# One-tile blocks for the first projection and wk, and another split of the PSUM banks, in a two-block network kernel

## The chip, the cores and the metric

The kernel runs on one core of a Trainium2 chip. The metric is the device time of one execution in microseconds (us). Engines are named as the profile names them: PE is TensorE (PEld its weight loads), DVE is VectorE, ACT is ScalarE, POOL is GpSimd, SP is SyncE, which issues the DMAs.

## The reference

256 tokens x of width 2048 and a memory of 256 rows go through two blocks of a network in float32. What the change touches is the first block's beginning:

```
u  = rms_norm(x) @ w_in                        # 2048 -> 42 column tiles of 128
a  = ssd_mixer(u[SSD part])                    # Mamba-2, two chunks of 128 tokens
b  = rwkv7_mixer(u[RWKV part])                 # 16 heads, a recurrence over 256 steps
x  = x + concat(a, b) @ w_out                  # w_outa: mix 0..7, w_outb: mix 8..15
k, v = rms_norm(mem) @ wk, rms_norm(mem) @ wv  # then cross attention, feed-forward
```

The second block (attention, a state-space layer, two more feed-forward matrices) follows; all matrices are streamed from HBM once. The recurrence of the RWKV mixer is computed in chunks, which needs inverses of triangular matrices.

## The kernel before, in words

**The stream.** `gemm` (L482 to L536) goes through one weight matrix after the other, in the order of `SEQ` (L74): w_in, wk, wv, w_outa, w_outb, wq, wo and so on. A matrix is cut into blocks of columns (`CUT_IN`, `CUT_K`, L71), a block into units of 1024 columns per partition, 512 KB each. `fetch` (L447) has SP issue a unit's DMA into one of three raw buffers, `prep` (L463) splits it: ACT casts the high part wh, DVE subtracts for the low part wl (four buffers of each). w_in has 96 units, wk 32, wv 32, w_outa and w_outb 16 each. For each column tile and each of the unit's k-steps TensorE makes the products wh x hi, wh x lo and wl x hi with the split activations; in the first blocks of a matrix (`WIDE`) the first two are one matmul of 512 columns. After its last unit a tile is evicted (`evac`).

**The mixers** run beside the stream as generators. After each tile of a unit `gemm` calls `step` (L419), which lets each generator go one piece on if a clock of the program's own (the meter) has come to its time; so a block of two tiles calls it twice per unit, a block of one tile once. The RWKV mixer has eight pairs of heads in four quarters, one after the other: `rwkv_prep` makes the operands (tiles gb, ga, pb), `rwkv_inv` (from L700) the inverse. There POOL copies ga into D, DVE transposes it to L, POOL does a forward substitution on W with T as its temporary (62 operations for a quarter), DVE transposes W into Wc (L732), and ia, ib, ic, id on TensorE finish it. `rwkv_out` (L777) then makes gkp, kt, b, z, s and y for two chunks and, after the norm of y, yT and the tile mix8 to mix15. The next quarter's substitution needs the T of the one before, which that quarter's ib, ic and id still use.

**The memory.** `hook_in` (L1430) runs after each unit of w_in. In the last ten units it loads and splits the 16 tiles of the memory (mem, mems on ACT and DVE) and has POOL sum their squares (accmem). The row of the memory's norm is made from memss<-ones (a matmul that sums over partitions), a small chain on DVE (memv, memt, memy) and memss<-memy (a matmul that spreads it). `evac_k` (L1509) needs that row: while it is missing, `Rows.__missing__` (L295) steps the mixers. In the same way `gemm` steps them while an activation (mix14, mix15 for w_outb) is missing.

**PSUM.** `banks` (L330) deals eight banks: n to the stream's sums (pool mm), 2 to pairs (pd), 6 - n to the mixers' other tiles (ps). Before, n is `NMM` = 4 from the start.

**The order.** A scheduler puts the program's instructions in a fixed order on each engine, from the order in which the code issues them and its own estimate of when each could run; on the chip each engine keeps that order. A row that waits holds up all rows behind it on its engine.

Of the kernel before, what the change touches and what calls it, by code (L numbers as in the profile page):

```python
# [23 lines left out]
NG, NM, NX = 42, 35, 6  # L24
NT, T2, NTM, KB = 6, 6, 8, 3

NMM, NMB, NMC = 4, 5, 7

WIDE = {"w_in": 8, "w1": 16, "w2a": 4, "w2b": 4, "w2c": 2, "w_out2": 4, "w_up": 22, "w_da": 4, "w_db": 4}


LIVE, OL, LAT, XS = 4, 4, 0.28, 1.0
# [11 lines left out]
def _blocks(widths, k):  # L44

    out, off = [], 0
    nk = k // P
    for w in widths:
        units, kc = [], 1024 // w
        for c in range(0, nk, kc):  # L50
            n = min(kc, nk - c)
            units.append((c, n, off))
            off += P * n * w
        out.append((w, units))
    return out, off


def _flat(w, widths):
# [3 lines left out]
    for width in widths:  # L62
# [5 lines left out]


CUT_D = [512] * 3 + [256, 128, 128]  # L70
CUT_IN = [512] + [256] * 20 + [512]  # L71
CUT_K = [256] * 8
CUT_O = [256] * 8
SEQ = [("w_in", range(len(CUT_IN))), ("wk", range(len(CUT_K))), ("wv", range(4)), ("w_outa", range(len(CUT_O))), ("w_outb", range(len(CUT_O))), ("wq", range(4)), ("wo", range(4)),  # L74
       ("w1", range(6)), ("w2a", range(4)), ("w1", range(6, 11)), ("w2b", range(4)),
# [3 lines left out]
WIDTHS = {  # L79
    "w_in": CUT_IN,  # L80
    "wk": CUT_K, "wv": [512] * 4, "w_outa": CUT_O, "w_outb": CUT_O, "wq": [512] * 4, "wo": [512] * 4,
    "w1": [512] * 16, "w2a": [512] * 4, "w2b": [512] * 4, "w2c": [512] * 4,
# [152 lines left out]
class Meter:  # L235
# [5 lines left out]
    def __init__(self):  # L241
        self.clk = dict.fromkeys(self.FIXED, 0.0)
        self.t = 0.0
# [58 lines left out]
class Net:  # L302
    def __init__(self, ctx, tc, io):
        self.meter = Meter()
        self.tc, self.nc, self.io, self.ctx = tc, Engines(tc.nc, self.meter), io, ctx
        pool = lambda name, bufs, **k: ctx.enter_context(tc.tile_pool(name=name, bufs=bufs, **k))
        self.cp = pool("const", 1)
        self.rawp = pool("raw", RAW)
        self.whp = pool("wh", AHEAD)
        self.wlp = pool("wl", AHEAD)  # L310
        self.gp = pool("g", NG)
        self.ap = pool("act", 16)
        self.mctx = ctx.enter_context(ExitStack())
        self.mp = self.mctx.enter_context(tc.tile_pool(name="m", bufs=NM, side="right"))
        self.tp = pool("tmp", NT)
        self.sp = pool("small", 8)
        self.banks(NMM, "a")
        self.ready, self.raws, self.nraw, self.nunit = [], {}, 0, 0
        self.units, self.dmas = [], []
        for name, blocks in SEQ:  # L320
            allb = _blocks(WIDTHS[name], KDIM[name])[0]
            for b in blocks:
                width, us = allb[b]
                for c0, n, off in us:
                    self.units.append((name, b, width, c0, n, off))
        self.sides, self.nside, self.busy = [], 0, {}
        self.ncell = 0
        self.R, self.C, self.outs = Rows(self), Rows(self), 0
# [153 lines left out]
    def gemm(self, name, acts, evac, blocks=None, moving_w=False, hook=None):  # L482
# [5 lines left out]
        for blk in (range(len(widths)) if blocks is None else blocks):  # L488
            width = widths[blk]
            wide = blk < WIDE.get(name, 0)  # L490
            base = sum(widths[:blk]) // P
# [858 lines left out]
def tile_net(ctx, tc, io, out):  # L1350
    m = Net(ctx, tc, io)
# [45 lines left out]
    ms = None  # L1397
# [24 lines left out]
    def halves():  # L1422
        for n, w in (("w0", 8), ("a0", 8), ("k_a", 8), ("conv_w", 48), ("conv_b", 12)):
            m.half[n] = t = m.cp.tile([P, w], F32, tag="half_" + n, name="half_" + n)
            m.ts(t, m.v(n, 0, w), 0.5, None, ALU.mult, e=nc.gpsimd)
        for n, w in (("mu_pw", 1), ("mu_pa", 1), ("mu_pg", 2), ("mu_r", 8), ("mu_k", 8), ("mu_v", 8)):
            m.half["1-" + n] = t = m.cp.tile([P, w], F32, tag="1-" + n, name="om_" + n)
            m.ts(t, m.v(n, 0, w), -1.0, 1.0, ALU.mult, ALU.add, e=nc.gpsimd)

    def hook_in(cnt):  # L1430
        nonlocal ms
        if cnt == 2:
            nc.sync.dma_start(m.cst, io["cst"])
            m.bones = m.cp.tile([P, P], F32R, tag="bones", name="bonesr")
            m.act(m.bones, m.c("bones"), AF.Copy)
        if cnt == 3:
            nc.sync.dma_start(m.vec, io["vec"])
            halves()
        if cnt < 8:
            for k in (2 * cnt + 6, 2 * cnt + 7):  # L1440
                xs.split(k)
            loads(2)
        j = cnt - 88
        if j == -2:
            ms = Source("mem", m.v("norm_mem_g", 0, 16), "mem", False)
        if j >= -2:
            for k in (2 * j + 4, 2 * j + 5):
                ms.load(k)
        if j >= 0:
            for k in (2 * j, 2 * j + 1):  # L1450
                ms.split(k)

    m.mix = [None] * 16
    m.xbc, m.zs, m.pg = [], [], [None, None]
# [11 lines left out]
    def evac_in(n, ps):  # L1466
# [35 lines left out]
        else:  # L1502
            m.xbc.append(m.ssd_conv(i if kind == "bc" else 4 + i, ps, rB))

    m.gemm("w_in", xs.acts, evac_in, hook=hook_in)
    xs = None
    m.kT = [None] * 16
# [33 lines left out]
    ms = None  # L1541
# [280 lines left out]
```

## Time and profile before

| | |
|---|---|
| median of 3 runs | 2919.66 us (2918.85 to 2920.1) |
| profiled execution | 2919.99 us, span 2917.7 us |
| mean granted clock of TensorE | 0.988 |
| PE, DVE, ACT, POOL busy | 97%, 70%, 49%, 12% of the span |

The profile is of one execution. Busy shares are of the span. A timeline's row has its start, its duration, the engine, the line, the operation and output <- inputs, and in brackets how long the engine had been idle before it and what released it. All helpers' instructions have one line (L266), so rows are read by their tiles' names, with buffer numbers left out.

### The profile page before, as it was taken

Reading aid. Unit: us, or ns where it says so; the run is one execution under the profiler, and the core shown is the slowest. Engines: PE = TensorE matmul, PEld = TensorE weight load, DVE = VectorE, ACT = ScalarE, POOL = GpSimd, SP = SyncE. Lnnn points to the kernel's source line nnn. Section 1 sums busy time; section 2 is a strip of 40 time slices with the busy share of each in tenths; the row PEclk is TensorE's granted clock in tenths of the full one; section 3 lists DMA queues with packets and bytes.
Section 4 is the critical chain, followed back from the end, with each engine's and each line's share of the span. In section 5 each row is a group of like instructions: output and inputs, shape, how many; then the busy total and the mean of one; then the engine's idle time right before and its main releaser. Section 6 shows DMA issues by size and latency. Waiting matters only on the chain.

```text
span 2917.7 us, 50239 instructions
## 1 busy us (share of the span) xinstructions
PE 2840.0 (97%) x19668; PEld 2598.8 (89%) x19668; DVE 2037.5 (70%) x3689; ACT 1423.4 (49%) x2251; POOL 357.4 (12%) x590
## 2 busy tenths in 40 slices
PE   8989998999999999999999989999999999999998
PEld 7989898799999889988888989999988888888887
DVE  7977885567668675565666788887777665577655
ACT  6554643344454554454455535453555444444444
POOL 4444352600000000000000051210000000000000
PEclk9999999999999999999999999999999999999999
DMA  6544444454545556566565544455555555555664
GB/s 214 177 141 137 148 155 129 145 185 130 171 148 173 188 182 193 188 188 191 186 192 180 184 148 142 160 159 174 181 188 187 188 188 187 190 187 183 191 188 145
DMA packets 146253, 504.17 MB, mean 173 GB/s; under 512 B 16352, under 2 KB 24800, under 8 KB 146016
## 3 DMA queue, kind: packets, MB, share of 16 engines
q1 hardware_dynamic: 146016, 500.96, 53.7%
q8 instruction: 154, 2.52, 0.3%
q14 instruction: 83, 0.68, 0.1%
HBM read 498.80 MB, written 2.10 MB: 172 GB/s over the span
## 4 chain that ended last, share of the span: by engine, by line
PE 78%; DVE 3%; POOL 1%; issue 1%; ACT 0%; DMA 0%; DVEq 0%; ACTq 0%; POOLq 0%
PE mm_w_up L266 17%; PE mm_w L266 12%; PE mm_w_in L266 7%; PE mm_w2a L266 5%; PE mm_w_db L266 4%; PE mm_w_da L266 4%; PE mm_w2c L266 4%; PE mm_w2b L266 4%; PE mm_wo L266 3%; PE mm_wq L266 3%; PE mm_w_out L266 3%; PE mm_wv L266 2%; PE mm_w_outa L266 2%; PE mm_w_outb L266 2%; PE mm_w_ba L266 2%; PE mm_wk L266 1%
## 5 line engine op out<-in xcount | busy, mean ns | idle before, releaser
L266 PE MATMUL mm_w_up<-xu,wh_w_up 128*128 128x512 f32 x1408 | 487.9, 397 | 0.0
L266 PE MATMUL mm_w_up<-xu,wl_w_up 128*128 128x256 f32 x1408 | 376.6, 280 | 0.0
L266 PE MATMUL mm_w<-xf,wh_w 128*128 128x512 f32 x1024 | 350.6, 392 | 0.0
L266 DVE TENSOR_TENSOR wl_w_up<-raw_w_up,wh_w_up 128x1024 fp32r<-128x1024 f32 x176 | 215.4, 1224 | 148.2 <-ACT wh_w_up L266 147.4
L266 PEld LDWEIGHTS mm_w_up<-xu,wh_w_up 128*128 128x128 f32 x1408 | 256.9, 188 | 54.7
L266 ACT CAST wh_w_up<-raw_w_up 128x1024 fp32r<-128x1024 f32 x176 | 184.8, 1050 | 236.0 <-PE mm_w_up L266 219.5
L266 PE MATMUL mm_w_in<-ins,wh_w_in 128*128 128x256 f32 (+1 forms) x1248 | 287.7, 317 | 5.7 <-DVE ins L266 5.7
L266 ACT CAST wh_w_in<-raw_w_in 128x1024 fp32r<-128x1024 f32 (+1 forms) x189 | 196.8, 1043 | 189.8 <-PE mm_w_in L266 104.4
L266 DVE TENSOR_TENSOR wl_w_in<-raw_w_in,wh_w_in 128x1024 fp32r<-128x1024 f32 (+1 forms) x189 | 241.7, 1283 | 57.2 <-ACT wh_w_in L266 56.7
L266 PEld LDWEIGHTS mm_w_up<-xu,wl_w_up 128*128 128x128 f32 x1408 | 265.6, 189 | 9.8
L266 PE MATMUL mm_w<-xf,wl_w 128*128 128x256 f32 x1024 | 273.4, 280 | 0.0
L266 PE MATMUL mm_w_in<-xb,wh_w_in 128*128 128x256 f32 x1472 | 268.4, 284 | 1.1 <-DVE in L266 1.1
L266 DVE TENSOR_TENSOR wl_w<-raw_w,wh_w 128x1024 fp32r<-128x1024 f32 x128 | 156.8, 1225 | 122.0 <-ACT wh_w L266 120.4
L266 PEld LDWEIGHTS mm_w_in<-xb,wh_w_in 128*128 128x128 f32 x1472 | 226.7, 190 | 5.7 <-issue 2.3
L266 PEld LDWEIGHTS mm_w_in<-ins,wh_w_in 128*128 128x128 f32 x1248 | 207.8, 194 | 17.6 <-DVE ins L266 5.7
L266 PEld LDWEIGHTS mm_w<-xf,wh_w 128*128 128x128 f32 x1024 | 186.8, 188 | 35.9
L266 PE MATMUL mm_w_in<-ins,wl_w_in 128*128 128x256 f32 x768 | 215.2, 288 | 2.4 <-DVE wl_w_in L266 2.4
L266 PE MATMUL mm_w_in<-xb,wl_w_in 128*128 128x256 f32 x736 | 206.3, 284 | 2.2 <-DVE wl_w_in L266 2.2
L266 ACT CAST wh_w<-raw_w 128x1024 fp32r<-128x1024 f32 x128 | 134.3, 1049 | 144.2 <-PE mm_w L266 123.0
L266 PEld LDWEIGHTS mm_w<-xf,wl_w 128*128 128x128 f32 x1024 | 192.4, 188 | 7.0
L266 PEld LDWEIGHTS mm_w_in<-ins,wl_w_in 128*128 128x128 f32 x768 | 149.0, 194 | 6.7 <-DVE wl_w_in L266 3.6
L266 POOL TENSOR_TENSOR tt<-st,st 128x256 f32<-128x256 f32 x16 | 13.9, 868 | 1081.9 <-DVE acc L266 1081.5
(1523 smaller groups left out, 7445.7 us busy)
## 6 DMA issues: line engine op xcount, KB each, us to landing
raw_w_in<-in_w_in_dram SPq DMA_DIRECT2D x187, 512.0 KB, 3.6
raw_w_up<-in_w_up_dram SPq DMA_DIRECT2D x176, 512.0 KB, 3.9
raw_w<-in_w_dram SPq DMA_DIRECT2D x128, 512.0 KB, 4.2
raw_w2a<-in_w2a_dram SPq DMA_DIRECT2D x48, 512.0 KB, 4.2
raw_w_da<-in_w_da_dram SPq DMA_DIRECT2D x44, 512.0 KB, 3.9
raw_w_db<-in_w_db_dram SPq DMA_DIRECT2D x42, 512.0 KB, 4.1
raw_w2b<-in_w2b_dram SPq DMA_DIRECT2D x40, 512.0 KB, 4.1
raw_w2c<-in_w2c_dram SPq DMA_DIRECT2D x40, 512.0 KB, 4.2
```

The source lines that it names most:

```text
L266: return f(o, *a, **k)
```

## The change

w_in: one block of 512 columns, then 40 of 128 and two of 256, in place of one of 512, 20 of 256 and one of 512. wk: one of 256 and 14 of 128, in place of eight of 256. The number of units stays, and `WIDE` is set so that the same 18 tiles are wide. The stream's sums have four banks in the first block and three from the second on; the mixers' pool ps gets two and then three. The 16 memory tiles are split behind units 92 to 95, four tiles behind each, in place of 88 to 95, two behind each, and loaded accordingly later.

```diff
--- before.py
+++ after.py
@@ -24,9 +24,9 @@
 NG, NM, NX = 42, 35, 6
 NT, T2, NTM, KB = 6, 6, 8, 3
 
-NMM, NMB, NMC = 4, 5, 7
-
-WIDE = {"w_in": 8, "w1": 16, "w2a": 4, "w2b": 4, "w2c": 2, "w_out2": 4, "w_up": 22, "w_da": 4, "w_db": 4}
+NMM, NMB, NMC = 3, 5, 7
+
+WIDE = {"w_in": 15, "w1": 16, "w2a": 4, "w2b": 4, "w2c": 2, "w_out2": 4, "w_up": 22, "w_da": 4, "w_db": 4}
 
 
 LIVE, OL, LAT, XS = 4, 4, 0.28, 1.0
@@ -68,8 +68,8 @@
 
 
 CUT_D = [512] * 3 + [256, 128, 128]
-CUT_IN = [512] + [256] * 20 + [512]
-CUT_K = [256] * 8
+CUT_IN = [512] + [128] * 40 + [256] * 2
+CUT_K = [256] + [128] * 14
 CUT_O = [256] * 8
 SEQ = [("w_in", range(len(CUT_IN))), ("wk", range(len(CUT_K))), ("wv", range(4)), ("w_outa", range(len(CUT_O))), ("w_outb", range(len(CUT_O))), ("wq", range(4)), ("wo", range(4)),
        ("w1", range(6)), ("w2a", range(4)), ("w1", range(6, 11)), ("w2b", range(4)),
@@ -314,7 +314,7 @@
         self.mp = self.mctx.enter_context(tc.tile_pool(name="m", bufs=NM, side="right"))
         self.tp = pool("tmp", NT)
         self.sp = pool("small", 8)
-        self.banks(NMM, "a")
+        self.banks(4, "a")
         self.ready, self.raws, self.nraw, self.nunit = [], {}, 0, 0
         self.units, self.dmas = [], []
         for name, blocks in SEQ:
@@ -1429,6 +1429,8 @@
 
     def hook_in(cnt):
         nonlocal ms
+        if cnt == 7:
+            m.banks(NMM, "n")
         if cnt == 2:
             nc.sync.dma_start(m.cst, io["cst"])
             m.bones = m.cp.tile([P, P], F32R, tag="bones", name="bonesr")
@@ -1440,15 +1442,15 @@
             for k in (2 * cnt + 6, 2 * cnt + 7):
                 xs.split(k)
             loads(2)
-        j = cnt - 88
+        j = cnt - 92
         if j == -2:
             ms = Source("mem", m.v("norm_mem_g", 0, 16), "mem", False)
-        if j >= -2:
-            for k in (2 * j + 4, 2 * j + 5):
+        for b in range(2 * j, 2 * j + 2) if j >= 0 else (j,) if j >= -2 else ():
+            for k in (2 * b + 4, 2 * b + 5):
                 ms.load(k)
-        if j >= 0:
-            for k in (2 * j, 2 * j + 1):
-                ms.split(k)
+            if b >= 0:
+                for k in (2 * b, 2 * b + 1):
+                    ms.split(k)
 
     m.mix = [None] * 16
     m.xbc, m.zs, m.pg = [], [], [None, None]
```

The change moves instructions. Three places are shown as the rows of an engine in their order; a name's last number is the buffer's, a row with x2 stands for two instructions alike.

TensorE, first projection's end and wk (mm_wk_B_T is the sum of tile T in block B, memss the memory's norm, yT, sg, ss, ic and pb pieces of the mixers). Before, around memss<-memy:

```order
L266 MATMUL mm_wk_1_0_5234<-mems12_4901,wh_wk_1_12_5281 128x256 x2
L266 MATMUL mm_wk_1_0_5234<-mems12_4901,wl_wk_1_12_5282 128x256
L266 MATMUL mm_wk_1_0_5234<-mems13_4907,wh_wk_1_12_5281 128x256
L266 MATMUL ic1_5020<-Q1_4428,ga20_2362 64x64 x2
L266 MATMUL ic1_5020<-Q1_4428,ga21_2363 64x64
L266 MATMUL pb6_4892<-cst_98,v6_4134 128x128 x2
L266 MATMUL ic1_5020<-Q1_4428,ga21_2363 64x64
L266 MATMUL ic1_5020<-Q1_4428,ga30_2532 64x64 x2
L266 MATMUL ic1_5020<-Q1_4428,ga31_2533 64x64 x2
L266 MATMUL memss_5133<-cst_98,memy_5139 128x128 x2
L266 MATMUL mm_wk_1_0_5234<-mems13_4907,wh_wk_1_12_5281 128x256
L266 MATMUL mm_wk_1_0_5234<-mems13_4907,wl_wk_1_12_5282 128x256
```

Now, around the same row:

```order
L266 MATMUL yT1_5015<-pg0h_537,lorg1h_4790 128x256
L266 MATMUL yT1_5015<-pg0l_538,lorg1h_4790 128x256
L266 MATMUL yT1_5015<-pg0h_537,lorg1l_4791 128x256
L266 MATMUL yT1_5015<-pg1h_556,lorg1h_4790 128x256
L266 MATMUL yT1_5015<-pg1l_557,lorg1h_4790 128x256
L266 MATMUL yT1_5015<-pg1h_556,lorg1l_4791 128x256
L266 MATMUL sg1ss_5168<-ones_99,sacc1_4984 128x1 x2
L266 MATMUL memss_4862<-cst_98,memy_4868 128x128 x2
L266 MATMUL ss5_5282<-cst_98,kq5_5109 128x2 x2
L266 MATMUL mm_wk_1_0_4919<-mems0_4360,wh_wk_1_0_4773 128x256 x2
L266 MATMUL mm_wk_1_0_4919<-mems0_4360,wl_wk_1_0_4774 128x256
```

Before, block 1 of wk lies around memss<-memy and between it and memss<-ones (53 rows earlier). Now memss<-ones is 42 rows earlier; between lie the last eight rows of block 0 and then pieces of the mixers alone, and block 1 begins behind it.

TensorE, the last quarter of the RWKV mixer. Before, its ic3 stands between w_outa's tiles:

```order
L266 MATMUL mm_w_outa_3_0_7822<-mix3_7402,wh_w_outa_3_0_7746 128x256 x2
L266 MATMUL mm_w_outa_3_0_7822<-mix3_7402,wl_w_outa_3_0_7747 128x256
L266 MATMUL ic3_7836<-Q3_7449,ga60_4997 64x64 x2
L266 MATMUL ic3_7836<-Q3_7449,ga61_4998 64x64 x2
L266 MATMUL ic3_7836<-Q3_7449,ga70_6531 64x64 x2
L266 MATMUL ic3_7836<-Q3_7449,ga71_6532 64x64 x2
L266 MATMUL mm_w_outa_3_1_7823<-mix0_7349,wh_w_outa_3_0_7746 128x256 x2
L266 MATMUL mm_w_outa_3_1_7823<-mix0_7349,wl_w_outa_3_0_7747 128x256
```

Now it comes in w_outb's block 0, behind the products with mix12 and mix13:

```order
L266 MATMUL mm_w_outb_0_1_8103<-mix12_8032,wl_w_outb_0_4_8063 128x256
L266 MATMUL mm_w_outb_0_1_8103<-mix13_8079,wh_w_outb_0_4_8062 128x256 x2
L266 MATMUL mm_w_outb_0_1_8103<-mix13_8079,wl_w_outb_0_4_8063 128x256
L266 MATMUL ib3_8173<-Q3_8118,T3_7203 32x32 x16
L266 MATMUL ib3_8173<-T3_7203,Q3_8118 32x32 x8
L266 MATMUL ic3_8201<-Q3_8118,ga60_5559 64x64 x2
L266 MATMUL ic3_8201<-Q3_8118,ga61_5560 64x64 x2
L266 MATMUL ic3_8201<-Q3_8118,ga70_6937 64x64 x2
L266 MATMUL ic3_8201<-Q3_8118,ga71_6938 64x64 x2
L266 MATMUL gkp60_8227<-rh6_5244,ka6_5241 128x128 x2
```

Before, ib3 to yT7 are spread from w_outa's block 1 to w_outb's block 1, three sums of w_outb being begun by then. Now the 73 rows from ib3 to yT7 are one run, and the next row of the stream is w_outb's product with mix14.

DVE, behind the second quarter's transpose Wc1 (gk, ce, m, zh are mixers' operands, wl the low part of a unit). Before:

```order
L266 STREAM_TRANSPOSE Wc1_4426<-W1_3392 128x1024
L266 SCALAR_TENSOR_TENSOR zh2_3836<-mm_w_in_18_0_3703,row_in_490 128x256
L266 TENSOR_TENSOR ce6_3814<-ce6_3814,xbc3_1447 128x256
L266 TENSOR_TENSOR m6_3809<-m6_3809,cbm_1455 128x512
L266 TENSOR_TENSOR gk010_3847<-gkp01_3840,cst_98 128x256
L266 SCALAR_TENSOR_TENSOR gk010_3847<-gkp01_3840,nn0_1107,cst_98 128x128
```

Now:

```order
L266 STREAM_TRANSPOSE Wc1_5187<-W1_3911 128x1024
L266 TENSOR_TENSOR wl_w_in_42_4_4277<-raw_w_in_42_4_4189,wh_w_in_42_4_4276 128x1024
L266 TENSOR_TENSOR m7_4219<-m7_4219,cbm_1429 128x512
L266 TENSOR_TENSOR wl_w_in_42_8_4321<-raw_w_in_42_8_4239,wh_w_in_42_8_4320 128x1024
L266 SCALAR_TENSOR_TENSOR zh4_4293<-mm_w_in_41_0_4163,row_in_490 128x256
```

Before, the first row behind Wc1 that TensorE needs next is gk010, four rows on; now it is wl_w_in_42_4, directly behind. The same holds for Wc2 (wl_wv_0_10, directly behind); behind Wc0 it is wl_w_in_23_8, eight rows on (before xe0, six on), behind Wc3 gk410, five rows on.

## Rows read from the trace of the kernel before

**Rows 1.** The page's first part: engine, busy us, share, instructions.

```profile
PE 2840.0 (97%) x19668; PEld 2598.8 (89%) x19668; DVE 2037.5 (70%) x3689; ACT 1423.4 (49%) x2251; POOL 357.4 (12%) x590
```

**Rows 2.** Waits of TensorE, 0 to 900 us: total us, times, longest.

```profile
PE b L266 <- DVE gk L266: 20.8, 3, 8.9
...
PE st L266 <- DVE xe L266: 7.7, 1, 7.7
...
PE gb L266 <- DVE M L266: 1.3, 1, 1.3
```

**Rows 3.** Timeline of DVE: first and last of the four transposes Wc.

```profile
171.18 1.25 DVE L266 STREAM_TRANSPOSE Wc<-W 128x1024 f32<-128x1024 f32 x1 [8.52 <-POOL W L266]
...
570.45 1.25 DVE L266 STREAM_TRANSPOSE Wc<-W 128x1024 f32<-128x1024 f32 x1 [10.57 <-POOL W L266]
```

**Rows 4.** Timeline of TensorE: the four long waits, and id ahead of three.

```profile
175.22 0.77 PE L266 MATMUL st<-xe,btok 128*128 128x128 f32 x2 [7.72 <-DVE xe L266]
...
248.07 1.14 PE L266 MATMUL id<-M,Q 64*64 64x64 f32 x16
...
305.48 0.69 PE L266 MATMUL b<-vt,gk 128*128 128x64 f32 x2 [5.93 <-DVE gk L266]
...
393.59 1.14 PE L266 MATMUL id<-M,Q 64*64 64x64 f32 x16
...
450.97 0.69 PE L266 MATMUL b<-vt,gk 128*128 128x64 f32 x2 [8.86 <-DVE gk L266]
...
516.21 1.14 PE L266 MATMUL id<-M,Q 64*64 64x64 f32 x16
...
573.19 1.28 PE L266 MATMUL b<-vt,gk 128*128 128x64 f32 x4 [6.03 <-DVE gk L266]
```

**Rows 5.** Windows: length, PE, PEld, DVE, ACT, POOL busy, granted clock, DMA share, GB/s.

```profile
175.00:178.50 3.50, 3.28 (x15) 3.31 (x16) 3.50 (x9) 3.44 (x8) 1.21 (x3) 0.50 0.62 192
...
691.00:694.00 3.00, 2.66 (x13) 2.69 (x14) 0.97 (x4) 0.24 (x2) 0.00 (x0) 0.50 0.03 5
...
700.00:704.00 4.00, 4.00 (x33) 4.00 (x32) 2.51 (x6) 2.64 (x5) 0.00 (x0) 0.91 0.00 0
```

**Rows 6.** Timeline of TensorE at the memory's norm and at the mixers' end.

```profile
391.57 0.71 PE L266 MATMUL memss<-cst,memy 128*128 128x128 f32 x4
...
648.11 0.49 PE L266 MATMUL gkp<-rh,ka 64*128 64x128 f32 x4
...
685.19 0.39 PE L266 MATMUL y<-al,gk 128*128 128x64 f32 x2
...
685.59 0.40 PE L266 MATMUL mm_w_outb<-mix,wh_w_outb 128*128 128x256 f32 x2
...
685.95 0.40 PE L266 MATMUL mm_w_outb<-mix,wh_w_outb 128*128 128x256 f32 x2
...
687.77 0.69 PE L266 MATMUL yT<-cst,ka 128*128 128x128 f32 x2 [0.59 <-DVE ka L266]
...
691.34 0.45 PE L266 MATMUL yT<-cst,ka 128*128 128x128 f32 x1 [2.18 <-DVE ka L266]
...
696.30 0.80 PE L266 MATMUL mm_w_outb<-mix,wh_w_outb 128*128 128x256 f32 x2 [1.10 <-DVE xin L266]
```

**Rows 7.** Timeline of DVE at the memory's norm.

```profile
382.62 0.15 DVE L266 TENSOR_SCALAR memv<-memss 128x2 f32<-128x2 f32 x1
...
387.47 0.42 DVE L266 TENSOR_TENSOR bon<-pb,v 128x256 f32<-128x256 f32 x1 [0.19 <-PE pb L266]
...
387.81 0.15 DVE L266 SCALAR_TENSOR_TENSOR memy<-memt,memy 128x2 f32<-128x2 f32 x1
```

**Rows 8.** Groups on DVE, 300 to 400 us: busy us, mean ns, idle before.

```profile
L266 DVE TENSOR_TENSOR wl_wk<-raw_wk,wh_wk 128x1024 fp32r<-128x1024 f32 x9 | 11.5, 1278 | 0.8 <-ACT wh_wk L266 0.8
...
L266 DVE SCALAR_TENSOR_TENSOR mems<-mem,vec,mems 128x256 fp32r<-128x256 f32 x16 | 10.6, 660 | 0.1
...
L266 DVE TENSOR_TENSOR gk<-gkp,cst 128x256 f32<-128x256 f32 x6 | 2.5, 411 | 0.0
```

## The prediction

> **What bounds the kernel.** I read first the busy shares: TensorE (PE) is busy 97% of the span, the next engine, VectorE (DVE), 70% [rows 1]. So the time is TensorE's work, which the change leaves as it is (as many units, matmuls, weight loads), plus what TensorE stands idle, plus what it runs at its lower clock. Second, the waits of TensorE in the first 900 us, the stretch that the change reorders: four waits hold 28.5 us, one at st for DVE's xe (7.7) and three at b for DVE's gk (20.8) [rows 2]. Third, the timelines around them. DVE stands in its queue at the transpose Wc<-W of a mixer's quarter, 8 to 12 us each time, until GpSimd (POOL) has finished the substitution W [rows 3]; what stands behind Wc in DVE's queue is late, and TensorE stops at the first of its rows that reads it. The last three quarters start when the quarter before has done id: from id's start to the row that waited there are 57.4, 57.4 and 57.0 us, in which TensorE had 51.5, 48.5 and 51.0 us of work [rows 4]. This length is POOL's and DVE's, and the change touches none of it. Last, the clock: behind such a wait the granted clock is 0.50, the 1.2 GHz level, for 3.5 us; behind the small waits at the mixers' end it is 0.50 too, and 0.91 again in 700 to 704 us [rows 5].
>
> The profiled execution took 2919.99 us, 0.3 above the median of the runs, so sums against it stand for the median too. 0.2% is 5.8 us; less than that a measurement of this kernel hardly tells from no change.
>
> **The change, part by part.** Blocks of one tile, the split of the wide tiles (18 before and after) and the later memory loads change no instruction's shape and no count. A k-step of three matmuls stays 0.36 us (685.59 to 685.95) [rows 6], a unit of eight 2.9 us. DMA: the 16 memory tiles of 128 KB come within four units in place of eight, and on SP's queue stand between weight units that are fetched three ahead; I count nothing for it, and 1 us if a unit lands late. The change of banks after block 0 makes block 1 wait for another old bank's eviction: 0 to 1 us, taken as 0. The price is in the order.
>
> *The four waits.* With one step of the mixers per one-tile block, a quarter spans other work. I price TensorE's rows from id to the first row that needs DVE's work behind Wc, at 0.36 us a k-step and the mixers' own rows at their spacing in the trace. Second quarter: 48.6 us before, 50.0 now. Third: 44.2, now 54.2. Fourth: 49.5, now 54.3. For the first, from the unit at which DVE reaches L: 51.4, now 55.3. So the waits lose 3.9, 1.4, 10.0 and 4.8 us. But the row that waits now reads a weight split (wl), not a small operand: behind Wc0 eight DVE rows come before it (4 us more), behind Wc1 and Wc2 one split (0.8 more each), behind Wc3 five rows (2 more). New waits: 7.7 - 3.9 + 4 = 7.8; 5.9 - 1.4 + 0.8 = 5.3; 8.9 - 10.0 + 0.8, so 0; 6.0 - 4.8 + 2 = 3.2. That is 16.3 in place of 28.5: **12 us saved**, and 1.8 us more for the wait that goes, half of its 3.5 us at the lower clock: -14. Bounds: nothing, and all 28.5 + 4 x 1.8 = 36.
>
> *The memory's norm.* Here I see the largest new cost. Before, between memss<-ones (the sum) and memss<-memy (the broadcast) TensorE had the end of block 0 of wk and most of a tile of block 1, 7.7 us, with some mixers' rows, and DVE's chain memv to memy took 5.2 us [rows 7]; the broadcast came at 391.57 without a wait [rows 6]. Now three banks are the stream's, block 0 of wk holds two of them until the row of the memory's norm is there, and between the two memss rows stand 1.4 us of wk and 4.6 us of mixers' rows, with no stream row behind ia1 until the broadcast is done. At the same place DVE's queue is denser: the 16 mems now come in four units, right behind Wc1. From Wc1 to memv I count 95 operations: 10 splits at 1.2, 16 mems at 0.66 (their mean beside POOL's adds, against 0.41 of a plain 256-wide one), 26 wide ones at 0.35 (0.34 from one start to the next), 43 small ones at 0.15 [rows 7, 8]: 38 us; from memv to the last memy 49 more, with one split and ten wide ones: 10. With the transpose the broadcast is possible some 50 us behind Wc1's start. TensorE starts again 2.5 us behind it, has 32.8 us of work up to the broadcast, and so would be there at 35. **14.5 us idle**, in pieces at memss, sgb0, yT1. Off go the waits that this place has now, of which gb's for M is 1.3 [rows 2]: some 2 in all. The clock falls in such a stretch as it did at 691 to 703 us; I take 1.5 us. Net **+14**; bounds +5 (if mems and adds don't meet, 0.41 each, and half of the small operations overlap) and +20.
>
> *A cluster in wv* (unit 139: z31, y21, y31, ia2, ib2, yT2 and others within 7 us of stream): the handoffs from TensorE to DVE and back take more than the rows between; 0 to 5, taken as +2.
>
> *The mixers' end.* w_outb's block 0 needs mix14 and mix15. Before, the last quarter's pieces from ic3 on were spread among the units of w_outa and w_outb, and the waits were 0.59 and 2.18 at yT and 1.10 at the xin add, 3.9 us [rows 6]. Now 24 pieces from ib3 to yT7 stand in one run with no stream row between, again while block 0 holds two of three banks: 18.4 us of TensorE's rows. The chain through them (ib, ic, id, then b, z, s, y for two chunks, each handed to ACT or DVE and back at about 1 us, DVE with 16 gk operations of 0.4 on the way, and the last y's norm, 5.8 us from its matmul at 685.5 to yT at 691.34 [rows 6]) comes to 28 to 29 us: 10 idle in place of 3.9. **+6**, the lower clock taken as before (about 10 us of it [rows 5]); bounds 0 and +14.
>
> Sum: -14 + 14 + 2 + 6 = **+8 us**: 2919.99 + 8 = 2928, slower by 0.3%.
>
> A rule on the clock speaks against the change. The row shows 0.50 for 3.5 us behind a long wait and for some 10 us around short ones [rows 5], so I took a few us. The Trainium skill, "TensorE: Matmul & The Clock Gate", Part 1, says that the half-rate state is the default and that activity releases it. By that rule the two runs without stream rows, which TensorE fills by two thirds, could stay throttled throughout, and the sum would be nearer the third rival's than mine.
>
> **Rivals.**
> 1. *The waits close* (faster). If the mixers' third bank and smaller steps give TensorE 57 us of its own rows between id and the first row behind Wc in every quarter, all 28.5 us go, with 7 us of lower clock; the runs at the norm and at the end cost half as much, +10, and wv +2: 2919.99 - 35.5 + 12 = 2896; if only three waits close, about 2905. For it: the third and fourth quarter gain 10 and 5 us of rows. Against: the releaser is DVE held by POOL [rows 3], not a bank, and splits now stand behind Wc. It decides at 57 us of rows. Chance 0.21. The Trainium skill, "Perfetto Trace Analysis", Identifying Performance Opportunities, says that the same gap repeating on the engine that should be saturated can mean too few PSUM buffers; by that rule this rival would be the case. The trace's releasers don't agree.
> 2. *They cancel* (no change). If DVE's mems overlap POOL's adds less, the norm costs +6 in place of 14: 2920. For it: DVE idles 30% of the span. Against: in its queue there is no idle place to use. Chance 0.27.
> 3. *The runs are dearer* (slower still). TensorE's 24 us of rows in both runs at 1.2 GHz, a third of it not hidden by the waits, +8, and each wait 2 longer: 2928 + 12 = 2940. Chance 0.12.
>
> **Numbers.** My own forecast, 2926 to 2936, has 0.40. Slower by over 0.2% is it and the third rival, 0.52; within 0.2%, 0.27; faster, 0.21. The range, 2904 to 2942, takes in the milder half of the first rival and most of the third, and the bounds of the norm and the end together.
>
> **What would show it.** In the waits of the changed kernel: mm_w_in or mm_wv waiting for wl behind Wc0 and Wc1 (8 and 5 us), b for gk at one place only; at the norm, sgb, yT and memss waiting for DVE, 12 to 16 us together, with DVE without idle from Wc1 on; at the end, ten or more waits of 0.3 to 3 us from ib to yT7. The forecast falls if TensorE's waits at the norm stay under 6 us, or if the four waits go altogether. In windows of 50 us the granted clock should be lowest there, under 0.90.

## The result and the profile after

The changed kernel takes **2942.5 us** (median of four runs, 2941.5 to 2944.41) against 2919.88 (2918.85 to 2920.69): a ratio of 1.0078, 95% interval 1.0061 to 1.0096, so slower by 0.8%, 22.6 us. The sign was forecast, the size was not: 2928 was said, with 2942 as the upper end. The profiled execution took 2941.5 us, with a span of 2939.7.

The first line of the page already splits the loss. The columns are those of [rows 1].

```profile
PE 2851.5 (97%) x19668; PEld 2607.6 (89%) x19668; DVE 2041.0 (69%) x3689; ACT 1420.2 (48%) x2251; POOL 358.4 (12%) x590
```

TensorE has the same 19668 matmuls as before, and its busy time has grown by 2851.5 - 2840.0 = 11.5 us. The same rows took longer, and that is its clock: the mean granted clock went from 0.988 to 0.982. The span grew by 22.0 us, so the other 10.5 are idle time. Half of the loss is thus invisible in a list of waits.

The waits of TensorE, 0 to 900 us (total us, times, longest), the view of [rows 2]:

```profile
PE mm_w_outa L266 <- DVE xin L266: 8.8, 1, 8.8
PE yT L266 <- DVE ka L266: 8.7, 5, 2.8
PE mm_w_in L266 <- DVE wl_w_in L266: 6.6, 3, 3.3
...
PE mm_w_in L266 <- DVE foldw_in L266: 6.2, 1, 6.2
PE sgb L266 <- DVE memt L266: 3.0, 1, 3.0
PE pb L266 <- DVE ql L266: 2.9, 2, 2.1
PE s L266 <- DVE al L266: 2.5, 2, 1.6
...
PE mm_wv L266 <- DVE wl_wv L266: 2.1, 1, 2.1
PE ib L266 <- DVE T L266: 1.6, 1, 1.6
PE z L266 <- ACT be L266: 1.5, 2, 1.1
```

Of the rows that waited before, b for gk (20.8) and st for xe (7.7) are gone. One long wait is left of four, at xin; there is a new one at foldw_in, and a dozen of 0.4 to 3 us at the norm, in wv and at the mixers' end. The windows of those places (columns as in [rows 5]):

```profile
0.00:50.00 50.00, 30.15 (x146) 24.12 (x147) 34.23 (x51) 32.31 (x67) 28.52 (x57) 0.90 0.69 217
168.00:202.00 34.00, 30.18 (x239) 28.12 (x238) 32.74 (x59) 17.64 (x37) 29.01 (x46) 0.95 0.37 119
338.00:348.00 10.00, 6.45 (x37) 5.69 (x35) 8.95 (x15) 4.49 (x12) 2.52 (x5) 0.66 0.48 162
364.00:396.00 32.00, 25.59 (x187) 24.55 (x186) 29.87 (x133) 15.58 (x39) 10.14 (x18) 0.73 0.27 88
502.00:506.00 4.00, 1.92 (x9) 1.25 (x8) 3.22 (x3) 0.00 (x0) 1.54 (x4) 1.00 0.00 0
524.00:538.00 14.00, 9.94 (x115) 8.64 (x114) 11.13 (x57) 2.88 (x7) 1.78 (x7) 0.64 0.00 1
628.00:642.00 14.00, 5.20 (x33) 4.66 (x31) 5.15 (x9) 1.05 (x1) 6.53 (x16) 0.63 0.23 69
680.00:720.00 40.00, 32.27 (x265) 29.63 (x264) 23.88 (x98) 9.01 (x27) 0.00 (x0) 0.70 0.09 31
```

A window's length less PE's busy time is what TensorE stood idle; its busy time multiplied by one minus the granted clock (the column behind POOL, 0.70 in the last row) is what the lower clock cost. The mean clock of a long window weighs idle time too, so I took both sums over windows of 2 us from 0 to 800 us and added them up by place. This ledger is used for all kernels below; "a+b" is idle plus lower clock, in us, good to some 0.3.

| place | before | after | difference | forecast |
|---|---|---|---|---|
| start, 0 to 50 | 12.3+1.6 | 19.9+1.9 | +7.9 | 0 |
| four waits at Wc | 28.8+8.9 | 18.2+5.9 | -13.6 | -14 |
| memory's norm | 2.2+1.6 | 6.4+6.7 | +9.3 | +14 |
| wv cluster | 0 | 4.1+3.8 | +7.9 | +2 |
| mixers' end | 3.9+4.1 | 7.7+9.3 | +9.0 | +6 |
| small waits elsewhere | 0.6 | 2.2 | +1.6 | 0 |
| all, 0 to 800 us | 48.0+16.2 | 58.5+27.9 | +22.2 | +8 |

The ledger explains the 22.0 us of the span; behind 800 us nothing differs.

**Start.** DVE and TensorE at the change of banks, timelines of the changed kernel, DVE first:

```profile
46.35 0.41 DVE L266 TENSOR_TENSOR foldw_in<-foldw_in,mm_w_in 128x256 f32<-128x256 f32 x1
```

```profile
46.82 0.80 PE L266 MATMUL mm_w_in<-ins,wh_w_in 128*128 128x512 f32 x1 [6.20 <-DVE foldw_in L266]
47.42 0.41 PE L266 MATMUL mm_w_in<-ins,wl_w_in 128*128 128x256 f32 x1
47.63 0.63 PE L266 MATMUL mm_w_in<-ins,wh_w_in 128*128 128x512 f32 x1
```

The foldw_in that TensorE waits for is the eviction (a fold is the addition of a wide tile's two halves) of the last of block 0's four tiles, not of the first. Before, TensorE began block 1 at 40.83 us without a wait, 7.5 us ahead of that last fold:

```profile
40.83 0.48 PE L266 MATMUL mm_w_in<-ins,wh_w_in 128*128 128x512 f32 x1
...
48.30 0.42 DVE L266 TENSOR_TENSOR foldw_in<-foldw_in,mm_w_in 128x256 f32<-128x256 f32 x1
```

Behind the wait the row after a 256-wide product starts 0.21 us behind it (47.42 to 47.63) and not 0.12; the granted clock is 0.50 from 46.8 to 50 us, the 1.2 GHz level.

**The four waits.** DVE's transposes Wc of the first, second and fourth quarter, and the last row of the memory's norm on DVE:

```profile
190.07 1.25 DVE L266 STREAM_TRANSPOSE Wc<-W 128x1024 f32<-128x1024 f32 x1 [1.26 <-POOL W L266]
...
339.06 1.25 DVE L266 STREAM_TRANSPOSE Wc<-W 128x1024 f32<-128x1024 f32 x1 [7.82 <-POOL W L266]
...
387.39 0.15 DVE L266 SCALAR_TENSOR_TENSOR memy<-memt,memy 128x2 f32<-128x2 f32 x1
...
634.70 1.25 DVE L266 STREAM_TRANSPOSE Wc<-W 128x1024 f32<-128x1024 f32 x1 [11.90 <-POOL W L266]
```

From the second quarter on DVE stands 8 to 12 us as before [rows 3], but TensorE has more of its own to do meanwhile. In the first quarter DVE hardly stands: 1.26 us for 8.52. It comes to that Wc 49 us after POOL began the substitution (139.98 us), in place of 41.5, when POOL is almost done. From the second Wc to the last memy are 387.54 - 339.06 = 48.5 us.

**Norm and end.** TensorE's waits at both, in order of time:

```profile
378.69 1.20 PE L266 MATMUL sgb<-cst,sg0y 128*128 128x128 f32 x4 [2.95 <-DVE memt L266]
...
385.70 0.45 PE L266 MATMUL yT<-cst,ka 128*128 128x128 f32 x1 [2.83 <-DVE ka L266]
...
389.43 1.20 PE L266 MATMUL memss<-cst,memy 128*128 128x128 f32 x4
...
693.58 0.49 PE L266 MATMUL s<-al,kbt 128*128 128x128 f32 x2 [1.56 <-DVE al L266]
...
706.47 0.83 PE L266 MATMUL yT<-cst,ka 128*128 128x128 f32 x2 [1.71 <-DVE ka L266]
...
710.24 0.89 PE L266 MATMUL yT<-cst,ka 128*128 128x128 f32 x2 [1.66 <-DVE ka L266]
```

The broadcast memss<-memy takes 1.20 us where it took 0.71 [rows 6], and comes without a wait, 1.9 us after the last memy was done (387.54): TensorE was slow enough that DVE was ready.

### The profile page after: what moved, and what is told of

It is laid out like the page before. It is cut to its first block, busy times and chain, and to the rows that moved or that the text cites. A ratio compares the mean times of both kernels' runs of the same rounds, so it can differ in the third digit from the quotient of the medians.

```text
span 2939.7 us, 50255 instructions
## 1 busy us (share of the span) xinstructions
PE 2851.5 (97%) x19668; PEld 2607.6 (89%) x19668; DVE 2041.0 (69%) x3689; ACT 1420.2 (48%) x2251; POOL 358.4 (12%) x590
## 4 chain that ended last, share of the span: by engine, by line
PE 84%; POOL 7%; DVE 5%; issue 2%; ACT 1%; DMA 1%; SPq 0%; DVEq 0%; POOLq 0%; ACTq 0%
PE mm_w_up L266 17%; PE mm_w L266 12%; PE mm_w_in L266 12%; PE mm_w2a L266 5%; PE mm_w_db L266 4%; PE mm_w_da L266 4%; PE mm_w2c L266 4%; PE mm_w2b L266 4%; PE mm_wo L266 3%; PE mm_wq L266 3%; POOL W L266 3%; PE mm_w_out L266 3%; POOL T L266 3%; PE mm_wk L266 2%; PE mm_wv L266 2%
## 5 line engine op out<-in xcount | busy, mean ns | idle before, releaser
L266 PEld LDWEIGHTS mm_w_in<-ins,wl_w_in 128*128 128x128 f32 x768 | 149.3, 194 | 10.8 <-DVE wl_w_in L266 8.6
L266 PEld LDWEIGHTS mm_w_in<-xb,wl_w_in 128*128 128x128 f32 x736 | 138.3, 189 | 5.3 <-DVE wl_w_in L266 2.7
```

The lines of the kernel that those rows point to most:

```text
L266: return f(o, *a, **k)
```

## The experiments

The theory after the result: three causes, each with its place. The change of banks makes block 1 wait for all of block 0's tiles (start). The cuts make the mixers late against the stream, so that their last pieces come without stream rows around them (wv, end). In such runs the clock falls and costs as much as the waits. The rivals: the three banks themselves cost (a bank is missing where TensorE waits); or one particular wait in the run drops the clock. Every experiment is a single run, beside a run of the kernel before on the same chip (its time stands in brackets), which took 2919.23 to 2922.46 us in the four groups; the changed kernel's own four runs lie 2.9 us apart. So time differences under some 3 us are not read, and the place of the loss in the ledger is what counts. The ledger's sums follow the times within 4 us.

### The change of banks

**The cuts with four banks throughout:** the change, without its third bank for the mixers and without the change of banks.

```diff
-NMM, NMB, NMC = 3, 5, 7
+NMM, NMB, NMC = 4, 5, 7
-        if cnt == 7:
-            m.banks(NMM, "n")
```

> The changed kernel with the stream's four PSUM banks kept throughout, so without the change of banks behind block 0; cuts and memory loads as changed. Theory A (the banks cost: the change of banks itself some 8 us at 40 to 50 us of the trace, and three banks leave the stream nothing to do at the memory's norm and at the mixers' end): the 6.2 us wait of mm_w_in for foldw_in is gone, and the runs without stream rows at the norm and at the end shrink; 2917 to 2928 us. Theory B (the cuts cost: one step of the mixers per one-tile block makes the mixers late, whatever the banks): only the change of banks goes, 2934 us or more, with the waits in wv and at the end as in the changed kernel.

Measured: 2932.2 us (before beside it 2921.28), between the two ranges: 10.9 of the 22.6 us stay, 11.7 go. Start 14.1, as before; norm 5.0; wv nothing; the end 6.5+15.0 = 21.5, the largest of all runs. So the start belongs to the banks, the end to the cuts. The norm (13.1 in the changed kernel) and wv (7.9) need the banks too: with four banks and as many steps as here the norm loses at most 5.0 in any run, and wv nothing.

**The change of banks alone, to the same sizes:** the kernel before (NMM stays 4), its PSUM pools closed and opened again behind the same unit.

```diff
+        if cnt == 7:
+            m.banks(NMM, "n")
```

> The kernel before with the pools of banks closed and opened again, at their old sizes, behind block 0. Theory A: the first tile of block 1 has to wait until all four tiles of block 0 are evicted, 5 to 6 us idle and 2 us at the lower clock at 40 to 50 us: 2926 to 2929 us. Theory B (the wait at 47 us comes from the one-tile block or the smaller pool): no wait there, 2920 us within 2.

Measured: 2927.2 us (2921.28), 5.9 slower, as expected; start 22.9, the end 2.8 and the norm 1.4 less than before, the rest the same. Its waits of TensorE have the row of after:

```profile
PE mm_w_in L266 <- DVE foldw_in L266: 5.1, 1, 5.1
```

Nothing but the closing and opening differs, with as many banks in each pool: the price is the handover, not a bank that is missing.

**The change of banks two units later,** with wk's cut undone:

```diff
-CUT_K = [256] + [128] * 14
+CUT_K = [256] * 8
-        if cnt == 7:
+        if cnt == 9:
```

> The changed kernel with wk in blocks of 256 and the change of banks behind block 1 (one tile in flight) in place of block 0 (four tiles). If the new pools wait for the tiles in flight to be evicted, the wait falls from 6.6 us to 1 to 2 us and the time from 2927 to 2920 to 2923 us. If changing banks costs the same wherever it stands: 2926 to 2929 us.

Measured: 2929.0 us (2922.46): missed. The wait is there again, 5.4 us at foldw_in, a block later, and the start lost 22.5. I had expected that one tile in flight would cost less than four. But its fold stood in DVE's queue behind those of block 0, the last of which came at 50.33 us, and started at 52.34, 5 us behind the tile's last product.

**Three banks from the start,** no change of banks, a first block of three tiles, wk's cut undone:

```diff
-CUT_IN = [512] + [128] * 40 + [256] * 2
-CUT_K = [256] + [128] * 14
+CUT_IN = [384] + [128] * 41 + [256] * 2
+CUT_K = [256] * 8
-        self.banks(4, "a")
+        self.banks(NMM, "a")
-        if cnt == 7:
-            m.banks(NMM, "n")
```

(w_in's wide blocks are 16, and the memory's tiles are split from unit 94 on, to go with it.)

> The kernel of wk_256 (w_in in one-tile blocks, wk as before) with a first block of 384 columns, so that the stream has three banks from the start and the banks are not changed. If the change of banks costs 6 us or more in that kernel too (2927): 2919 to 2922 us, with no wait for foldw_in at 47 us. If a first block of three tiles leaves TensorE idle while x comes in: what it wins is given back before 40 us, 2926 us or more.

Measured: 2925.3 us (2919.23), between the two ranges. Start 18.5, half way. TensorE's timeline shows what is left:

```profile
36.04 0.79 PE L266 MATMUL mm_w_in<-ins,wh_w_in 128*128 128x512 f32 x1 [3.87 <-DVE foldw_in L266]
...
45.87 0.47 PE L266 MATMUL mm_w_in<-ins,wh_w_in 128*128 128x512 f32 x1 [1.09 <-DVE foldw_in L266]
```

With three banks block 1 waits for the fold of the first tile, 3.9 us: DVE is late with the folds at the start in every arrangement, and four banks without a change are what hid it.

### The cuts

**Both cuts undone,** the banks left as changed:

```diff
-CUT_IN = [512] + [128] * 40 + [256] * 2
-CUT_K = [256] + [128] * 14
+CUT_IN = [512] + [256] * 22
+CUT_K = [256] * 8
```

(`WIDE` goes with it, here and wherever w_in's cut changes.)

> The changed kernel with blocks of 256 columns again in w_in (the first of 512 stays, the last 512 stays cut in two) and in wk, eight wide blocks; banks and memory loads as changed. Theory A (banks): the wait behind block 0 stays, and the norm and the end stay bad: 2932 to 2942 us. Theory B (cuts): the four long waits come back as before, and only the 8 us behind block 0 stay: 2924 to 2929 us.

Measured: 2933.4 us (2921.28), in the range of theory A, but the waits are those of theory B. Start 21.7; the four waits are long again (8.9, 8.9, 11.2, 8.0 with their clock); norm 8.9, end 6.1. With the old cuts the banks give nothing back: the mixers' third bank does not shorten the waits, w_in's cut does.

**wk's cut undone:**

```diff
-CUT_K = [256] + [128] * 14
+CUT_K = [256] * 8
```

> The changed kernel with wk in blocks of 256 again. If the losses at the norm, in wv and at the end come from wk's one-tile blocks (half as many steps, so the mixers fall behind and are forced later), they fall by half or more: 2925 to 2932 us. If they come from the banks and from w_in's cut, the time stays at 2938 to 2946 us.

Measured: 2927.3 us (2921.28), 15 us less than the changed kernel. The wv cluster is gone, the end is 4.5+2.4, the waits as in after; the norm, at 12.8, did not fall as I had expected. So behind w_in's cut and the three banks wk's cut is worth 15 us of the 22.

**w_in's cut alone,** on the kernel before:

```diff
-CUT_IN = [512] + [256] * 20 + [512]
+CUT_IN = [512] + [128] * 40 + [512]
```

> The kernel before with only w_in's middle cut to 40 blocks of 128 (first and last block of 512, 15 wide blocks, memory loads, four banks and wk as before). Theory W (w_in's one-tile blocks shorten the four long waits, some 13 us; wk's one-tile blocks and the change of banks cost the rest): 2904 to 2912 us. Theory M (one-tile blocks make the mixers late wherever they stand, so that the waits won are given back in wv and at the end): 2918 to 2930 us, with more than 10 us lost to waits and clock from 660 us on.

Measured: 2922.4 us (2922.46): no difference. The four waits at Wc fall by some 9 us and the norm's 3.8 go, but a handful of smaller waits of 0.5 to 2.2 us (st, wa, pb, z, ys) come in between, some 10 us with their clock, and the end takes 6 more (6.0+8.0).

**wk's cut alone,** on the kernel before:

```diff
-CUT_K = [256] * 8
+CUT_K = [256] + [128] * 14
```

> The kernel before with only wk cut into one block of 256 and 14 of 128. Theory W: the mixers fall behind in wk, and the losses appear in wv and at the end without any other part of the change, 15 us more: 2930 to 2939 us. If wk's cut costs only together with w_in's or with three banks: 2918 to 2925 us.

Measured: 2924.4 us (2922.46): theory W missed; alone it costs 2 (5 by the ledger), not the 15 that it costs behind w_in's cut and three banks. The third wait falls from 10.8 to 6.1 and the end rises to 13.9.

**Four banks and wk's cut undone:** the first experiment with wk's old cut.

```diff
-NMM, NMB, NMC = 3, 5, 7
+NMM, NMB, NMC = 4, 5, 7
-CUT_K = [256] + [128] * 14
+CUT_K = [256] * 8
-        if cnt == 7:
-            m.banks(NMM, "n")
```

> The changed kernel without the change of banks and with wk in blocks of 256: what is left of it is w_in's cut, its last 512 columns as two blocks of 256, and the memory's loads behind the last four units. Theory W: 2932 less 15 of wk's cut, 2915 to 2919 us, above the one with w_in's middle cut alone by what the crowded norm costs (5 to 9 us). If the norm's loss needs three banks: within 3 us of that kernel.

Measured: 2927.9 us (2922.46): missed by 9. Start 14.7 and norm 2.2 are cheap, but the end is 8.5+8.1 = 16.6 and the rest 35.7. Against w_in's middle cut alone it is 5.4 slower: that is the price of the last block's split and the memory's later loads together. Against this kernel the first experiment adds wk's cut, which so costs some 5.5 with four banks, between the 2 alone and the 15 with three.

Two pairs differ by the banks alone: this kernel and the one with wk's cut undone, and the first experiment and the changed kernel. In both the change of banks adds 7 to 8 us at the start and 8 to 11 at the norm, and takes 7.5 to 8 off the rest (35.7 to 28.0, 34.1 to 26.6) and 10 or 4.5 off the end. So behind w_in's cut the third mixers' bank is worth something, about what the change of banks costs at the start; the norm, and wv where wk is cut, come on top.

### Whether the mixers' lateness sets the end

**A step in the middle of a unit,** in blocks of one tile, so that the mixers get as many calls as with two tiles:

```diff
                             nc.tensor.matmul(o, a, b, start=first and q == 0, stop=last and q == len(ops) - 1)
+                        if nt == 1 and k == m // 2 - 1:
+                            mt.t = mt.now()
+                            self.step()
                     mt.t = mt.now()
```

> The changed kernel with a second step of the mixers in the middle of a unit of a one-tile block, so that a unit calls it twice as before. Theory L (one step per unit makes the mixers late: third id at 579 us in place of 516, so that the last quarter falls into w_outb's block 0): third id before 550 us, the loss in wv (8 us) gone and that at the end down from 17 to 10 us or less; 2924 to 2932 us. If the lateness comes from the order of w_in's tiles and the banks, not from the steps: third id within 10 us of 579, 2938 us or more.

Measured: 2933.8 us (2919.23), 1.8 above the range. As theory L says, the third quarter's id comes at 532 us and not at 579, the wv cluster is gone, the end falls from 17.0 to 9.2. But the long waits are back:

```profile
PE b L266 <- DVE gk L266: 11.9, 3, 6.1
PE wa L266 <- DVE xbc L266: 8.9, 1, 8.9
```

DVE, too, stands at the first Wc again, 7.18 us for 1.26. So lateness goes with both the saving at the waits and the loss at the end: mixers that run late leave stream rows to cover POOL's substitution, and have few left at w_outb.

**The same step with w_in's cut alone:**

> The kernel before with w_in's middle cut alone (2922) and the second step in the middle of a unit. Theory L: the end's loss falls from 14 to 9 us or less, the third id comes before 540 us (551 without); 2915 to 2920 us. Rival (with as many steps as before the long waits come back too): 2919 to 2923 us, the four long waits back to 30 us of idle and clock or more.

Measured: 2928.0 us (2919.23), against 2922.4 without the step: above both ranges. End 5.1, start 14.6, but four waits of 9 to 12 and 7.5 at the norm. The early mixers cost more than they give.

**The same step with three banks from the start** (and wk's cut undone):

> Three banks from the start, wk as before, and the second step in the middle of a unit in w_in's one-tile blocks. Theory L: no loss behind block 0, the end at 7 us or less, the norm at 13 us or less: 2910 to 2918 us, below both kernels. Rival: the long waits come back, 2919 to 2926 us.

Measured: 2932.9 us (2919.23): missed by 15, and 7 above the rival's range. Long waits again (11.3, 8.8, 9.0, 9.1), norm 10.9, end 8.6. So a third bank for the mixers does not close the four waits.

### The norm

**wk's first block of one tile:**

```diff
-CUT_K = [256] + [128] * 14
+CUT_K = [128] * 16
```

> The changed kernel with wk's first block, too, of 128 columns, so that one of the three banks and not two is held until the row of the memory's norm is there. Theory A (the held banks empty the stream there): stream rows stand between the two memss rows, the loss at the norm falls from 13 us to 3 to 7; 2932 to 2937 us. If DVE's crowded queue alone sets the norm's end and TensorE waits for it anyway (at the stream's weights in place of memss): 2940 us or more.

Measured: 2929.6 us (2920.56), faster than either range. Stream rows now lie between the two memss, and the norm loses 8.6 in place of 13.1, not the 3 to 7 of theory A. Most of what is left waits at the first memss, for POOL's sums:

```profile
375.29 1.01 PE L266 MATMUL memss<-ones,accmem 128*128 128x1 f32 x4 [4.36 <-POOL accmem L266]
```

wv kept its 7.7. The end fell to 7.3, though the edit was not aimed at it: a dozen stream matmuls now lie between ib3, ic3 and id3. From id3 to yT7 there is still not one, so the missing stream rows are not the end's whole cause; what else is, this run does not show. The wait of s for al is gone.

**wk in one tile, seven pairs and one tile; and z copied by ACT** (below):

```diff
-CUT_K = [256] + [128] * 14
+CUT_K = [128] + [256] * 7 + [128]
-            nc.vector.tensor_copy(z, pt[:, :P])
+            self.act(z, pt[:, :P], AF.Copy)
```

> w_in as changed and the change of banks, wk in one block of 128, seven of 256 and one of 128, and z's copy on ACT. If the losses are independent (2927 with wk of 256, less 6 to 10 at the norm, less 0 to 3 at the end): 2915 to 2921 us. If the last wait in w_outa (8.8 us) grows by what is won: 2923 us or more.

Measured: 2922.6 us (2920.56): 1.6 above the range, but the best kernel that still changes the banks. Start 21.7, norm 10.6, no wv cluster, end 6.2.

### What drops the clock at the end

In the changed kernel the clock falls at 695 us, behind the wait of s for al (693.58). If that wait did it, z's copy on ACT, which takes DVE out of the chain ahead of it, should keep the clock up.

```diff
-            nc.vector.tensor_copy(z, pt[:, :P])
+            self.act(z, pt[:, :P], AF.Copy)
```

> The changed kernel with z's copy out of PSUM in the output of the RWKV mixer done by ACT in place of DVE, where it stands behind the gk operations and makes TensorE wait 1.6 us at s (693.6 us). Theory C (that wait drops TensorE's clock in the middle of the run without stream rows, and the later small waits keep it at 0.50 for 24 us: 9 of the 17 us lost at the end): the wait at s is under 0.6 us, the clock falls later, the end's loss is 8 to 11 us; 2933 to 2937 us. If the lower clock comes with the run itself, whatever its waits: the loss stays at 15 us or more, 2940 us or more.

Measured: 2947.2 us (2920.56): theory C is wrong, the kernel is slower than the changed one. The wait at s fell from 1.56 to 0.37, and the end lost 6.7+13.6. (The edit also made the scheduler order the mixers' rows there anew, so it did not take away the wait alone.) The windows of the run, of the changed kernel first, then of this one:

```profile
680.00:692.00 12.00, 11.02 (x162) 9.76 (x160) 7.63 (x21) 2.44 (x7) 0.00 (x0) 1.00 0.24 78
692.00:716.00 24.00, 17.25 (x83) 15.87 (x82) 13.89 (x70) 5.00 (x16) 0.00 (x0) 0.57 0.04 12
```

```profile
683.00:687.00 4.00, 3.32 (x42) 2.92 (x40) 1.81 (x4) 0.73 (x2) 0.00 (x0) 1.00 0.45 154
687.00:707.00 20.00, 19.63 (x105) 17.57 (x104) 9.04 (x33) 3.38 (x12) 0.00 (x0) 0.50 0.05 14
707.00:711.00 4.00, 3.78 (x29) 3.44 (x27) 1.60 (x11) 0.82 (x4) 0.00 (x0) 0.93 0.01 2
```

Here the clock fell by 687 us, behind a wait of 0.68, and stayed at 0.50 for 20 us in which TensorE was busy for 19.6. No single wait explains that. A busy TensorE at the lower level hides its loss from every list of waits: no row of this stretch has a wait over 0.4 us. Nor does the run without stream rows explain it. With wk's cut undone 132 stream matmuls lie among ib3, but from ic3 (675.71 us) to yT7 there is none, and the clock holds until the last pieces all the same:

```profile
672.00:692.00 20.00, 18.86 (x198) 17.21 (x198) 12.80 (x41) 5.28 (x14) 0.00 (x0) 1.00 0.31 93
692.00:704.00 12.00, 8.33 (x45) 6.94 (x44) 9.24 (x52) 3.00 (x8) 0.00 (x0) 0.72 0.04 11
```

And with both cuts and four banks, the first experiment, the run begins with the same rows as in the changed kernel, ib3 and then ic3 behind the same wait of 0.61 us for Q. There the clock is at 0.50 from 672 us on, in the changed kernel (second window) it stays at 1.00:

```profile
672.00:685.00 13.00, 12.90 (x82) 11.28 (x81) 5.58 (x18) 1.20 (x5) 0.00 (x0) 0.50 0.00 1
```

```profile
683.00:692.00 9.00, 8.63 (x96) 7.58 (x95) 5.57 (x18) 1.57 (x5) 0.00 (x0) 1.00 0.19 67
```

So the size of the end's loss goes with how early in the run the clock falls, and what makes it fall early or late is not shown.

**The same copy on the kernel with w_in's cut alone:**

> The kernel with w_in's middle cut alone (2922) and z's copy on ACT. Theory C: of its 14 us lost at the end 4 to 7 go; 2915 to 2919 us, below both kernels. If the clock there falls anyway: 2920 to 2924 us.

Measured: 2921.0 us (2920.56). The end falls from 14.0 to 4.9+5.4 = 10.3, the time by less than a single run can tell. No kernel here beats the one before.

The runs that take the change apart, by the ledger: sums of idle and lower clock in us. The start is counted until the clock is back at 1.00 (up to 58 us), the rest is mostly the four waits:

| kernel | start | norm | wv | end | rest | all | time |
|---|---|---|---|---|---|---|---|
| before | 13.9 | 3.8 | 0 | 8.0 | 38.5 | 64.2 | 2919.9 |
| change of banks alone | 22.9 | 2.4 | 0 | 5.2 | 38.8 | 69.3 | 2927.2 |
| both cuts undone | 21.7 | 8.9 | 0 | 6.1 | 38.5 | 75.2 | 2933.4 |
| w_in's cut alone | 12.2 | 0 | 0 | 14.0 | 40.2 | 66.4 | 2922.4 |
| wk's cut alone | 14.8 | 3.8 | 0 | 13.9 | 36.9 | 69.4 | 2924.4 |
| both cuts, four banks | 14.1 | 5.0 | 0 | 21.5 | 34.1 | 74.7 | 2932.2 |
| w_in's cut and banks | 21.9 | 12.8 | 0 | 6.9 | 28.0 | 69.6 | 2927.3 |
| after | 21.8 | 13.1 | 7.9 | 17.0 | 26.6 | 86.4 | 2942.5 |

## Why the prediction was wrong

**The step that failed first is the change of banks**, "0 to 1 us, taken as 0". It measured +7.9 in the changed kernel, and 5.9 us of time when done alone. I had thought of it as a wait for another old bank's eviction; it is a wait for the last of all tiles in the old pools. The trace of before had the price: DVE's folds at the start came behind many rows, and the last fold of block 0 was to be read there, not the first. With this term alone the sum would have been 2936, in the range. The ledger's 22.2 us lie 14.2 above the forecast's 8: 7.9 of them at the start, 5.9 in wv, 3.0 at the end, 1.6 in small waits and 0.4 at the four waits, less 4.7 at the norm.

**wv and the end were mis-sized.** The places and kinds of wait were right (yT for ka, s for al, z for be, ib for T), as was the chain: 28 to 29 us were forecast from ib3 to yT7, and 680.06 to 711 is 31. But wv measured +7.9 where I took 2 (0 to 5), and the end +9.0 where I took 6. In both the lower clock is the larger part of the error: 3.8 us in wv, where I had counted none, and 9.3 at the end, where I had taken it "as before", at 4.1 by the ledger. The end's idle time grew by 3.8, less than the 6 forecast, in seven waits and not ten or more.

**The four waits were right in sum,** -13.6 for -14, idle 18.2 for 16.3, but by luck: errors cancel. The first cost 3.8 idle for 7.8, the second 3.5 for 5.3, the third 2.1 for 0, the fourth 8.8 for 3.2. At the first the mechanism was wrong: "8 to 12 us each time" did not hold, since DVE stood 1.26 us there. Behind that Wc TensorE waited only 0.80 us (pb<-ql at 200.43); the largest of the 3.8, 2.14 at pb<-ql (170.82), comes before DVE reaches it. At the fourth TensorE did not get as far as b<-gk: w_outa's next tile waits for the eviction xin, which stands behind Wc3 and a split. With four banks the wait is at b<-gk, 8.5 us long. So there three banks moved the wait and did not change its length. I had looked for the first row that reads an operand from behind Wc, and not for the first that needs a bank emptied behind it.

**The norm had the right length and the wrong price.** From Wc to the broadcast 50 us were forecast; 48.5 to the last memy and 50.4 to the broadcast were measured, but it costs 6.4 idle and 6.7 of clock, +9.3 for +14. What TensorE lost to the lower clock it did not wait, and in the end DVE was ready 1.9 us before it. By the prediction's own sign (TensorE's waits there under 6 us) the forecast fell: 2.95 at sgb and 2.83 at yT are 5.8, and memss did not wait. Its sign by the clock came true (0.83 from 350 to 400 us, 0.81 from 700 to 750). That this place needs the three banks, as the prediction says, the runs show: 13.1 and 12.8 with them, 5.0 and 2.2 without.

**The third rival's number was the nearest, by luck.** It priced the lower clock in the two runs at +8 and each wait 2 longer, 2940 us. The ledger has +11.7 of clock in all, 10.3 of it in those two runs; but the norm and the end together cost 18.3, less than the 20 of the forecast and the 32 of this rival, and the start and wv, which it did not have, made up the time. The Trainium skill, "TensorE: Matmul & The Clock Gate", Part 1, says that half rate is the default and that activity releases it, which I had weighed and left out of the sum. The trace agrees in part: the run at the end was not throttled from its first row (1.00 from 680 to 692 us, TensorE 92% busy) but later (0.57 over 692 to 716, 72% busy). It doesn't tell why 19.6 busy us of 20 stayed at 0.50 with z on ACT.

**The first rival fell** as a matter of banks. The rule of the Trainium skill, "Perfetto Trace Analysis", Identifying Performance Opportunities, that a gap which repeats can mean too few PSUM buffers, doesn't hold for these four gaps: with a third mixers' bank and old cuts, or with early mixers and three banks from the start, all four stay at 8 to 12 us. Only behind w_in's cut did the third bank take some 7.5 us off the rest.

What stays open: what exactly lowers the clock in these runs, and so why the end costs 7 us in one and 21 in another; how wv comes to need both wk's cut and the three banks; and the later loads of the memory alone, which weren't tried, since the loads go with the cut of w_in's last block (5.4 us together).

## What to carry to other kernels

Closing and opening PSUM pools in mid-stream made TensorE wait for the evictions of everything in flight, 5.1 to 7.0 us in every kernel here that did it; read the last of them on the evicting engine before you call it free. Pieces moved to a place without stream rows can pay twice, once in handoffs and once at half rate (7.7 and 9.3 us at the changed kernel's end), and the second does not show in the waits but in busy time that grows without one more instruction. The prices of edits do not add: w_in's cut with its later loads cost 5.4 us, wk's cut alone 2, the change of banks alone 5.9, and all together 22.6.

## What was not expected of the hardware

The granted clock cost as much as the idle time: 11.7 of 22.2 us. TensorE at 0.50 with 19.63 of 20 us busy (z on ACT, 687 to 707 us) shows that short waits are no sign of the higher level; with the 1.56 us wait of the changed kernel removed the stretch at 0.50 came earlier. Runs that begin with the same rows behind the same wait of 0.61 us went at 0.50 in one kernel (12.90 of 13 us busy) and at 1.00 in another. A single long wait was cheaper: 8.80 us of idle before xin were followed by only 1.6 us of loss to the clock, where the end's seven waits of 0.4 to 1.7 us, 7.7 together, were followed by 9.3.
